# Row sums scaled by a constant: smaller last jobs, an even split of the columns, early stores and two load queues

## Chip, cores, metric

One core of one Trainium2 chip. The metric is the device time of the whole program in microseconds (us); lower is better. Engines have the profile's names: DVE is the vector engine, ACT the scalar engine, SP the sync engine that issues DMAs (a q after a name is an engine's instruction queue). The profile's "span" is the time from the first to the last instruction of one profiled execution, some 1.8 us less than the metric.

## The reference

```python
batch, seq, dim = 32, 512, 1024           # x: 67.1 MB of float32, normal random numbers
def reference(x, multiplier):             # multiplier = 0.5
    return (np.sum(x, axis=-1) * multiplier).astype(np.float32)
```

The 16384 rows of 1024 numbers lie as 128 columns on each of 128 partitions. A column below is one number of the result on each partition, from 128 x 4 KB of input.

## The kernel before

```python
    G = 4
    NT = TPP // G                          # TPP = 128 columns, 32 jobs of four
    x_view = x_flat.rearrange("(p g j) d -> g p j d", p=P, j=G)
    NDVE = (NT * 17) // 32                 # 17 jobs on DVE, 15 on ACT
    BUFS = 10
    # ... pools, sums_dve, sums_act, scaled_dve; order: DVE and ACT jobs in turn, a DVE job last ...
    for g in order:
        x_tile = xpool.tile([P, G, D], fp32)
        nc.sync.dma_start(out=x_tile, in_=x_view[g])
        if g < NDVE:
            nc.vector.reduce_sum(out=sums_dve[:, g * G : (g + 1) * G], in_=x_tile,
                                 axis=mybir.AxisListType.X)
        else:
            for j in range(G):
                c = (g - NDVE) * G + j
                nc.scalar.activation(out=x_tile[:, j, :], in_=x_tile[:, j, :],
                    func=mybir.ActivationFunctionType.Copy, scale=float(multiplier),
                    accum_out=sums_act[:, c : c + 1])
    nc.vector.tensor_scalar(out=scaled_dve, in0=sums_dve, scalar1=float(multiplier),
                            scalar2=None, op0=mybir.AluOpType.mult)
    nc.sync.dma_start(out=out_view[:, : NDVE * G], in_=scaled_dve)
    nc.sync.dma_start(out=out_view[:, NDVE * G :], in_=sums_act)
```

## Time and profile before

| | kernel before |
|---|---|
| time, median of the first 5 runs | 168.96 us (168.85 to 169.38) |
| span of the profiled run (its time: 169.4) | 167.6 us |
| loads | 32 of 2.1 MB, one each 4.895 us |
| last load landed | 160.5 us |
| tail from there to the end of the span | 7.1 us |

The lines of the profile are in the prediction. The way to read them: find the stretch that is set by one resource (here the DMA engines, full from 3 us to 159 us: from 4.2 to 158.5 us at a share of 1.01 and 429 GB/s), then look only at what happens outside it.

### The profile page before, as it was taken

To read this page: it belongs to the slowest core of one execution; us is meant where nothing else is said; L and a number is where in the kernel's file an instruction comes from. 1 tells how busy PE (TensorE), PEld (TensorE's weight loads), DVE (VectorE), ACT (ScalarE), POOL (GpSimd) and SP (SyncE) were. 2 spreads that over 40 slices of the span, in tenths; PEclk is the share of its full clock that TensorE was granted. 3 is DMA by queue.
4 is the path that set the end of the run, shared out by engine and by line. 5 is a ranking of instruction groups with operands and counts; after the bars stand their busy time and mean duration, and the time that the engine had idled before them with its cause. 6 is when DMAs were issued, how large, how long until landed. Compare 5 with 4: busy or idle time off the path is not lost.

```text
span 167.6 us, 253 instructions
## 1 busy us (share of the span) xinstructions
DVE 75.3 (45%) x18; ACT 65.2 (39%) x121; POOL 0.2 (0%) x4
## 2 busy tenths in 40 slices
DVE  0090633709063370906328081552808155180884
ACT  3008155180814518082450906336090633609000
POOL 0000000000000000000000000000000000000000
DMA  5999999999999999999999999999999999999900
GB/s 184 430 430 430 434 422 430 430 434 434 422 430 422 426 434 430 430 422 430 422 432 430 430 426 430 430 422 430 434 426 426 430 426 426 434 426 434 394 8 8
DMA packets 4897, 67.18 MB, mean 401 GB/s; under 512 B 800, under 2 KB 800, under 8 KB 800
## 3 DMA queue, kind: packets, MB, share of 16 engines
q1 hardware_dynamic: 4896, 67.18, 94.6%
q14 instruction: 1, 0.01, 0.0%
HBM read 67.11 MB, written 0.07 MB: 401 GB/s over the span
## 4 chain that ended last, share of the span: by engine, by line
DMA 93%; DVE 3%; SPq 2%; issue 0%
DMA x_tile<-in_x_dram 93%; DVE sums_dve L58 3%; SPq L56 2%; DVE scaled_dve L74 0%
## 5 line engine op out<-in xcount | busy, mean ns | idle before, releaser
L58 DVE TENSOR_REDUCE sums_dve<-x_tile 128x4 f32<-128x4096 f32 x17 | 75.1, 4420 | 89.8 <-DMA x_tile<-in_x_dram 89.8
L66 ACT ACTIVATE x_tile<-x_tile 128x1024 f32<-128x1024 f32 x60 | 62.6, 1043 | 89.1 <-DMA x_tile<-in_x_dram 89.1
L66 ACT ACTIVATION_READ_ACCUMULATOR x_tile<-x_tile 128x1 f32 x60 | 11.2, 186 | 0.0
L66 ACT ACT_TABLE_LOAD x1 | 1.3, 1283 | 0.7 <-PEq L100 0.7
L74 DVE TENSOR_SCALAR scaled_dve<-sums_dve 128x68 f32<-128x68 f32 x1 | 0.2, 196 | 0.0
L100 POOL MEMSET const-bfloat16-1.0<- 128x1 bf16 x1 | 0.1, 101 | 0.0
L100 POOL MEMSET const-uint8-127<- 128x1 uint8 x1 | 0.1, 101 | 0.0
L100 POOL MEMSET const-float32-0.0<- 128x1 f32 x1 | 0.1, 98 | 0.2 <-issue 0.2
L100 POOL MEMSET const-float32-1.0<- 128x1 f32 x1 | 0.1, 98 | 0.0
## 6 DMA issues: line engine op xcount, KB each, us to landing
x_tile<-in_x_dram SPq DMA_DIRECT2D x32, 2048.0 KB, 39.1
out_dram<-scaled_dve SPq DMA_DIRECT2D x1, 34.0 KB, 1.5
out_dram<-sums_act SPq DMA_DIRECT2D x1, 30.0 KB, 5.6
```

Source lines behind the costliest of these rows:

```text
L56: nc.sync.dma_start(out=x_tile, in_=x_view[g])
L58: nc.vector.reduce_sum(out=sums_dve[:, g * G : (g + 1) * G], in_=x_tile, axis=mybir.AxisListType.X,)
L66: nc.scalar.activation(out=x_tile[:, j, :], in_=x_tile[:, j, :], func=mybir.ActivationFunctionType.Copy, scale=float(multiplier), accum_ou ...
L74: nc.vector.tensor_scalar(out=scaled_dve, in0=sums_dve, scalar1=float(multiplier), scalar2=None, op0=mybir.AluOpType.mult,)
L100: nc = _bacc.Bacc("TRN2", target_bir_lowering=False, num_devices=1)
```

## The change

Its intent: shorten what remains after the last load. Each engine gets 64 columns, and its last four come as jobs of 2, 1 and 1 columns. Each engine's sums are stored in two halves, each as soon as it is ready, ACT's from ACT's own DMA queue. Four of the first eight loads are issued by ACT. Cut to its core:

```diff
-    NDVE = (NT * 17) // 32
+    DVE_COLS = TPP // 2
+    ACT_COLS = TPP - DVE_COLS
+    def job_widths(total, bulk):
+        tail = [2, 1, 1] if total >= bulk * 2 + 4 else []
         ...                               # the rest in jobs of four
+    # jobs: DVE and ACT in turn, an ACT column last
+    CHUNK = 32
+    def flush(eng, upto_abs):             # stores 32 columns as soon as they are summed
+        ...
+            if eng == "v":
+                nc.vector.tensor_scalar(out=out_dve[:, lo:hi], in0=sums_dve[:, lo:hi],
+                                        scalar1=mult, scalar2=None, op0=mybir.AluOpType.mult)
+                nc.sync.dma_start(out=out_view[:, lo:hi], in_=out_dve[:, lo:hi])
+            else:
+                nc.scalar.dma_start(out=out_view[:, lo:hi],
+                    in_=sums_act[:, lo - DVE_COLS : hi - DVE_COLS])
     for ji, (eng, c0, w) in enumerate(jobs):
-        nc.sync.dma_start(out=x_tile, in_=x_view[g])
+        dma_eng = nc.scalar if (ji < 8 and ji % 2 == 1) else nc.sync
+        dma_eng.dma_start(out=x_tile, in_=x_cols[:, c0 : c0 + w, :])
         ...
+        flush(eng, done_cols[eng])
-    nc.vector.tensor_scalar(out=scaled_dve, ...)
-    nc.sync.dma_start(out=out_view[:, : NDVE * G], in_=scaled_dve)
-    nc.sync.dma_start(out=out_view[:, NDVE * G :], in_=sums_act)
```

More of the change, by code (lines that the diff above doesn't have):

```diff
@@ L25 @@
     TPP = T // P
-    G = 4
-    NT = TPP // G
-    assert TPP % G == 0
     x_flat = x.rearrange("b s d -> (b s) d")
-    x_view = x_flat.rearrange("(p g j) d -> g p j d", p=P, j=G)
+    x_cols = x_flat.rearrange("(p c) d -> p c d", p=P)
     out_view = out.rearrange("b s -> (b s)").rearrange("(p t) -> p t", p=P)
-    NDVE = (NT * 17) // 32
-    BUFS = 10
-    xpool = ctx.enter_context(tc.tile_pool(name="xpool", bufs=BUFS))
-    spool = ctx.enter_context(tc.tile_pool(name="spool", bufs=1))
-    sums_dve = spool.tile([P, NDVE * G], fp32)
@@ L44 @@
-    sums_act = spool.tile([P, (NT - NDVE) * G], fp32)
-    scaled_dve = spool.tile([P, NDVE * G], fp32)
-    order = []
-    for i in range(max(NDVE, NT - NDVE)):
-        if i < NDVE:
-            order.append(i)
-        if NDVE + i < NT:
-            order.append(NDVE + i)
-    for g in order:
-        x_tile = xpool.tile([P, G, D], fp32)
-        nc.sync.dma_start(out=x_tile, in_=x_view[g])
-        if g < NDVE:
+    DVE_COLS = TPP // 2
+    ACT_COLS = TPP - DVE_COLS
+    def job_widths(total, bulk):
+        tail = [2, 1, 1] if total >= bulk * 2 + 4 else []
+        bulk_cols = total - sum(tail)
+        ws = [bulk] * (bulk_cols // bulk)
+        rem = bulk_cols % bulk
+        if rem:
+            ws.append(rem)
+        return ws + tail
@@ new lines @@
+    GB = 4
+    dve_w = job_widths(DVE_COLS, GB)
+    act_w = job_widths(ACT_COLS, GB)
+    dve_jobs = []
+    c = 0
+    for w in dve_w:
+        dve_jobs.append(("v", c, w))
+        c += w
+    act_jobs = []
+    c = DVE_COLS
+    for w in act_w:
+        act_jobs.append(("a", c, w))
+        c += w
+    jobs = []
+    for i in range(max(len(dve_jobs), len(act_jobs))):
+        if i < len(dve_jobs):
+            jobs.append(dve_jobs[i])
+        if i < len(act_jobs):
+            jobs.append(act_jobs[i])
@@ new lines @@
+    CHUNK = 32
+    xpool = ctx.enter_context(tc.tile_pool(name="xpool", bufs=1))
+    spool = ctx.enter_context(tc.tile_pool(name="spool", bufs=1))
+    sums_dve = spool.tile([P, DVE_COLS], fp32)
+    out_dve = spool.tile([P, DVE_COLS], fp32)
+    sums_act = spool.tile([P, ACT_COLS], fp32)
+    BULK_BUFS = 10
+    SMALL_BUFS = 2
+    mult = float(multiplier)
+    done_cols = {"v": 0, "a": 0}
+    next_flush = {"v": CHUNK, "a": DVE_COLS + CHUNK}
+    def flush(eng, upto_abs):
+        while next_flush[eng] <= upto_abs:
+            hi = next_flush[eng]
+            lo = hi - CHUNK
+            if eng == "v":
+                nc.vector.tensor_scalar(
+                    out=out_dve[:, lo:hi],
+                    in0=sums_dve[:, lo:hi],
+                    scalar1=mult,
+                    scalar2=None,
+                    op0=mybir.AluOpType.mult,
+                )
+                nc.sync.dma_start(out=out_view[:, lo:hi], in_=out_dve[:, lo:hi])
+            else:
+                nc.scalar.dma_start(
+                    out=out_view[:, lo:hi],
+                    in_=sums_act[:, lo - DVE_COLS : hi - DVE_COLS],
+                )
+            next_flush[eng] += CHUNK
@@ L58 @@
+    for ji, (eng, c0, w) in enumerate(jobs):
+        if w == GB:
+            name, nbufs = "x_bulk", BULK_BUFS
+        else:
+            name, nbufs = "x_bulk", BULK_BUFS
+        x_tile = xpool.tile([P, w, D], fp32, name=name, bufs=nbufs)
+        dma_eng = nc.scalar if (ji < 8 and ji % 2 == 1) else nc.sync
+        dma_eng.dma_start(out=x_tile, in_=x_cols[:, c0 : c0 + w, :])
+        if eng == "v":
             nc.vector.reduce_sum(
-                out=sums_dve[:, g * G : (g + 1) * G],
+                out=sums_dve[:, c0 : c0 + w],
@@ L63 @@
         else:
-            for j in range(G):
-                c = (g - NDVE) * G + j
+            for j in range(w):
+                c = c0 + j - DVE_COLS
                 nc.scalar.activation(
@@ L69 @@
                     func=mybir.ActivationFunctionType.Copy,
-                    scale=float(multiplier),
+                    scale=mult,
                     accum_out=sums_act[:, c : c + 1],
                 )
-    nc.vector.tensor_scalar(
-        out=scaled_dve,
-        in0=sums_dve,
-        scalar1=float(multiplier),
-        scalar2=None,
-        op0=mybir.AluOpType.mult,
-    )
-    nc.sync.dma_start(out=out_view[:, : NDVE * G], in_=scaled_dve)
-    nc.sync.dma_start(out=out_view[:, NDVE * G :], in_=sums_act)
+        done_cols[eng] = c0 + w
+        flush(eng, done_cols[eng])
 _INS = ['x', 'multiplier']
```

## The prediction

> **What bounds the kernel now.** I read the page first: the tenths by slice and the chain that ended last.
>
> ```profile
> DVE  0090633709063370906328081552808155180884
> ACT  3008155180814518082450906336090633609000
> DMA  5999999999999999999999999999999999999900
> GB/s 184 430 430 430 434 422 430 430 434 434 422 430 422 426 434 430 430 422 430 422 432 430 430 426 430 430 422 430 434 426 426 430 426 426 434 426 434 394 8 8
> DMA 93%; DVE 3%; SPq 2%; issue 0%
> ```
>
> DMA is full in every slice but the first and the last two (a slice is 4.19 us), and 93% of the chain is loads. DVE and ACT are busy some 45% and 39% and only follow the landings. So there are three stretches: a start without data, a plateau that is set by the bytes, and a tail without data. Only the first and the last can give time back, or the plateau can be made longer. Next I read the end in the timeline, in order of time.
>
> ```profile
> 155.07 0.35 SPq L83 DMA_DIRECT2D out_dram<-sums_act  x1
> 155.62 4.42 DVE L58 TENSOR_REDUCE sums_dve<-x_tile 128x4 f32<-128x4096 f32 x1 [5.37 <-DMA x_tile<-in_x_dram]
> 160.51 4.42 DVE L58 TENSOR_REDUCE sums_dve<-x_tile 128x4 f32<-128x4096 f32 x1 [0.48 <-DMA x_tile<-in_x_dram]
> 164.97 0.20 DVE L74 TENSOR_SCALAR scaled_dve<-sums_dve 128x68 f32<-128x68 f32 x1
> 165.19 0.34 SPq L82 DMA_DIRECT2D out_dram<-scaled_dve  x1
> ```
>
> The last two loads both belong to DVE (17 jobs against ACT's 15), so the last load lands at 160.5 and then one engine alone reduces four columns for 4.42 us, multiplies for 0.20 us and has the sums stored. The page's list of DMA issues gives that store 1.5 us from issue to landing, so it lands at 166.7; the span ends at 167.6, 0.9 us later. The tail from the last landing is 167.6 - 160.5 = 7.1 us.
>
> Then the durations of the two engines, from the groups, and how one ACT job of four columns runs, from the timeline:
>
> ```profile
> L58 DVE TENSOR_REDUCE sums_dve<-x_tile 128x4 f32<-128x4096 f32 x17 | 75.1, 4420 | 89.8 <-DMA x_tile<-in_x_dram 89.8
> L66 ACT ACTIVATE x_tile<-x_tile 128x1024 f32<-128x1024 f32 x60 | 62.6, 1043 | 89.1 <-DMA x_tile<-in_x_dram 89.1
> ```
>
> ```profile
> 150.78 1.06 ACT L66 ACTIVATE x_tile<-x_tile 128x1024 f32<-128x1024 f32 x1 [5.53 <-DMA x_tile<-in_x_dram]
> 151.75 0.19 ACT L66 ACTIVATION_READ_ACCUMULATOR x_tile<-x_tile 128x1 f32 x1
> ...
> 153.92 1.04 ACT L66 ACTIVATE x_tile<-x_tile 128x1024 f32<-128x1024 f32 x1
> 154.86 0.19 ACT L66 ACTIVATION_READ_ACCUMULATOR x_tile<-x_tile 128x1 f32 x1
> ```
>
> One ACT column is over 151.94 - 150.78 = 1.16 us after its start; each further one adds 1.04 us. DVE starts 9.79 us apart (two loads), so one load of 2.1 MB takes 4.895 us, one column of 0.52 MB 1.22 us. Both engines need less for a column than the DMA does for one.
>
> Last, the start and end of the data, in a table of windows.
>
> ```profile
> 1.50:2.00 0.50, 0.00 (x0) 0.50 (x1) 0.00 (x0) 1.00 1.57 295
> 2.50:3.00 0.50, 0.00 (x0) 0.00 (x0) 0.00 (x0) 1.00 0.08 33
> 3.00:3.50 0.50, 0.00 (x0) 0.00 (x0) 0.00 (x0) 1.00 1.01 426
> 158.50:159.00 0.50, 0.50 (x1) 0.00 (x0) 0.00 (x0) 1.00 0.79 332
> 159.00:159.50 0.50, 0.50 (x1) 0.00 (x0) 0.00 (x0) 1.00 0.32 79
> ```
>
> The columns at the end are DMA share and GB/s. Packets begin after 1.5 us, 0.8 us or more after the first issue at 0.73, and the plateau begins at 3.0. In the trace's single packet records the first 16 KB packet of each engine takes 1.0 to 1.6 us and all later ones 0.61 us, so the start loses about 0.7 us beyond the wait for the first packet. Most engines end near 159.1, the slowest at 160.03; its semaphore frees DVE at 160.5.
>
> [...] The trace agrees that there is little to save: an issue takes 0.38 to 0.79 us in the chain, a load 4.895 us. [...]
>
> **The change, part by part.**
>
> *Smaller last jobs, balanced.* Each engine's last four columns become jobs of 2, 1 and 1. The loads end with DVE one column, then ACT one column. Call the last landing T. ACT's two-column job landed about 4.9 us before T and takes 2.2, its next column landed 2.4 before T, so ACT is idle at T: 1.16 us of work, then its store. DVE's last column landed at T - 1.22, is reduced by T, and its multiply (0.20) and store come well before ACT's. Tail: 1.16 (ACT) + 0.04 (two handovers like those between 164.95 and 165.19) + 1.5 (store to landing) + 0.9 (landing to end) = 3.6 us instead of 7.1: -3.5 us.
>
> *Smaller packets.* Columns lie one behind the other, so the rows of the last loads are 8 KB and 4 KB instead of 16 KB. In the packet records a 240-byte packet of the old store comes every 14 ns on one engine and a 16 KB packet every 611 ns; the line through these has a fixed part of 5 ns. Each engine moves 24 more packets for the 4 KB rows and 8 more for the 8 KB rows: 32 x 5 = 0.16 us. Four more loads each bring a 9 ns semaphore packet: 0.04 us. So +0.2 us.
>
> *Early stores.* A first half of each engine's sums (128 rows of 128 bytes) is stored during the plateau. The old ACT store had 8 packets per engine at 14 ns, 0.11 us with its semaphore packet 0.12; two of them +0.25 us on the DMA path. The final stores keep the size class of the old one. The added multiply of 0.2 us lies in DVE's idle time.
>
> *A store on the load queue.* The comparison of instruction orders puts DVE's first store on SP behind 13 SP loads, so that SP stands until DVE has finished job 14 and multiplied: about 4.42 + 0.25 us after that landing. By my walk through the waits, loads 15 and 16 are already issued then, 9.8 us of data. Load 15 is nearly through, load 16 covers 4.9 us; SP needs 0.35 us for the store, 0.45 for the next load and about 1 us to its first packet. About 3 us are to spare: 0.
>
> *Four early loads issued by ACT.* Loads 1 and 3 go out at the start, 5 and 7 (by the order) only after ACT's first eight columns, near 27 us. [...] the first two should land together near 12.5 us. The plateau's bytes and rate stay. Buffers and waits on the eighth load back leave SP always at least two loads ahead: 0. Nothing forces the first data earlier, as SP's first issue is where it was: 0.
>
> Sum: -3.5 + 0.2 + 0.25 = -3.05 us; 168.96 - 3.05 = 165.9 us, or -1.8%.
>
> **The rivals.**
>
> *The two queues hide the start.* If a second queue's packets overlap the slow first packet of each engine, up to 0.7 us comes back: 165.2 us, over 2% faster. For it: 1.0 to 1.6 us against 0.61 looks like latency, which overlap can hide. Against it: later packets are back to back with no gap, the engine appears to work on one at a time, and SP alone had several loads queued behind the first one.
>
> *The stores or the ordering open a bubble.* If the DVE store in the SP queue starves the loads, or if the small packets cost far more beside loads than alone, some 1 to 4 us are lost: 166.9 to 169.9 us. For it: SP does stand, and every load that waits for a slot can pass that on. Against it: 3 us of slack, and the old ACT store already went through behind a load with 14 ns a packet.
>
> *ACT's store is dearer than SP's.* ACT issued no DMA before. If its issue to landing is 2 to 2.5 us instead of 1.5, the time is 166.4 to 166.9. No view speaks to it.
>
> **Range and chances.** The mechanism of the tail is nearly certain; what is open is about half a microsecond each in the start, the plateau and ACT's store. 165.9 us, range 165.1 to 166.8. The 2% line is at 165.6, only 0.3 us below the centre, so faster is 0.35, same 0.63, slower 0.02.
>
> **What would show it.** Right: the last activation starts near 160.9 and is one column; ACT's store is the last thing issued, near 162.1; the span ends near 164.5; the plateau still shows about 428 GB/s with no slice below 9 tenths but the ends; DVE's first reduce starts near 12.5. Wrong: a slice in the middle (about 80 us) with less DMA; a last landing above 161.5 (plateau longer than the 0.45 us that I add) or below 160.3 (start gained); an ACT store with more than 2 us to landing; DVE's chain ending after ACT's.

## The result, and the profile after

The changed kernel took 165.86 us (median of 8 runs, 165.59 to 166.01); the kernel before took 169.29 us in the same rounds (15 runs, 168.85 to 169.49). The ratio is 0.980, with a 95% interval of 0.9788 to 0.9811. It lies on the 2% line, so the verdict between "faster" and "same" is unclear. Ratios here are the mean time of one kernel's fast runs over that of the other's of the same rounds, so they are not quite the ratio of the medians quoted. The time is the predicted 165.9 almost to the digit, but that flatters the prediction: the kernel before was 0.33 us slower in these rounds than in the five runs I started from. The drop is 3.4 us, predicted were 3.05.

The page of the changed kernel's profile, with busy tenths of each engine by slice and the chain that ended last:

```profile
DVE  0008247906346090642808246090642708145541
ACT  3007236009056708145090642708145090632872
DMA  5999999999999999999999999999999999999990
GB/s 192 432 440 420 436 428 440 424 424 436 420 432 428 424 428 432 436 420 422 440 420 425 436 424 428 436 420 432 432 420 432 428 432 428 424 436 404 412 372 8
DMA 93%; DVE 3%; SPq 2%; ACT 1%; issue 0%; ACTq 0%
```

The DMA row ends with one empty slice instead of two: the tail is shorter. In the middle no slice falls below nine tenths, so the early stores opened no bubble. The GB/s of slices 37 and 38 (404 and 412) show the small rows of the last loads; experiment 4, which has none, shows 432 in both. The end, from the timeline (start, duration, engine and line; in brackets how long the engine had been idle and what ended that):

```profile
159.06 1.22 DVE L113 TENSOR_REDUCE sums_dve<-x_bulk 128x1 f32<-128x1024 f32 x1 [1.34 <-DMA x_bulk<-in_x_dram]
160.31 0.18 DVE L88 TENSOR_SCALAR out_dve<-sums_dve 128x32 f32<-128x32 f32 x1
160.36 1.06 ACT L121 ACTIVATE x_bulk<-x_bulk 128x1024 f32<-128x1024 f32 x1 [1.38 <-DMA x_bulk<-in_x_dram]
160.52 0.34 SPq L95 DMA_DIRECT2D out_dram<-out_dve  x1
161.32 0.19 ACT L121 ACTIVATION_READ_ACCUMULATOR x_bulk<-x_bulk 128x1 f32 x1
161.54 0.35 ACTq L97 DMA_DIRECT2D out_dram<-sums_act  x1
```

ACT's last column starts at 160.36, at the landing, and its store is issued 1.18 us later; the span ends at 163.8, 2.3 us after that. The tail is 163.8 - 160.4 = 3.4 us, against 7.1 before. DVE, which ended the kernel before, is now done a microsecond ahead of ACT. Its one-column reduce takes 1.22 us; that it would be over at the last landing was my estimate, as the kernel before has only reduces of four columns (4.42 us).

The stand of SP that the order of instructions announced (its queue holds back loads until DVE has finished the sums that it must store) is there too (a wait of 24.4 us for DVE in SP's list of waits), in the timeline near 81 us:

```profile
81.33 0.18 DVE L88 TENSOR_SCALAR out_dve<-sums_dve 128x32 f32<-128x32 f32 x1
81.54 0.35 SPq L95 DMA_DIRECT2D out_dram<-out_dve  x1
81.94 13.36 SPq L110 DMA_DIRECT2D x_bulk<-in_x_dram  x7
```

SP's next load leaves 0.4 us after the store, while load 16 is still in the queue; the window from 80 to 85 us has a DMA share of 1.00 and 426 GB/s. The stand costs nothing.

What does not fit is the last landing: 160.4 in place of the 160.9 that the prediction worked out. Every term that was to lengthen the plateau is therefore in doubt, and the experiments take them one by one.

### The profile page after: what moved, and what is told of

Same layout as the page of the kernel before. It is cut to its first block, busy times and chain, and to the rows that moved or that the text cites. A ratio compares the mean times of both kernels' runs of the same rounds, so it can differ in the third digit from the quotient of the medians.

```text
span 163.8 us, 268 instructions
## 1 busy us (share of the span) xinstructions
DVE 71.4 (44%) x20; ACT 69.7 (43%) x129; POOL 0.2 (0%) x4
## 2 busy tenths in 40 slices
DMA packets 5761, 67.19 MB, mean 410 GB/s; under 512 B 1152, under 2 KB 1152, under 8 KB 1664
## 4 chain that ended last, share of the span: by engine, by line
DMA 93%; DVE 3%; SPq 2%; ACT 1%; issue 0%; ACTq 0%
DMA x_bulk<-in_x_dram 93%; DVE sums_dve L113 3%; SPq L110 1%; ACT x_bulk L121 1%; SPq L95 0%; DVE out_dve L88 0%; ACTq L121 0%
## 5 line engine op out<-in xcount | busy, mean ns | idle before, releaser
L113 DVE TENSOR_REDUCE sums_dve<-x_bulk 128x4 f32<-128x4096 f32 (+2 forms) x18 | 71.0, 3946 | 89.0 <-DMA x_bulk<-in_x_dram 89.0
L121 ACT ACTIVATE x_bulk<-x_bulk 128x1024 f32<-128x1024 f32 x64 | 66.8, 1044 | 90.1 <-DMA x_bulk<-in_x_dram 90.1
L121 ACT ACTIVATION_READ_ACCUMULATOR x_bulk<-x_bulk 128x1 f32 x64 | 11.9, 186 | 0.0
```

What stands on the lines that cost most here:

```text
L113: nc.vector.reduce_sum(out=sums_dve[:, c0 : c0 + w], in_=x_tile, axis=mybir.AxisListType.X,)
```

## The experiments

They ran in three groups of four, each group on one chip together with the kernel before (medians there 169.09, 169.14 and 169.21 us). Between groups I compare ratios only. Below, "jump" means: the last load's landing signal comes from 16 DMA engines (the trace has 16 semaphore updates for each load); the jump is how far the slowest comes behind the second slowest, from the trace's semaphore records. "Spread" is from the first engine's to the slowest's.

### 1. The small last jobs, with the even split, alone

Based on the changed kernel:

```diff
-        dma_eng = nc.scalar if (ji < 8 and ji % 2 == 1) else nc.sync
+        dma_eng = nc.sync
-    CHUNK = 32
+    CHUNK = 64
```

> The small, balanced last jobs alone: all loads from SP, one store per engine at the end (ACT's still from ACT). Theory (the tail gives everything, the early stores cost 0.25 us, two load queues gain 0.2 us at the start): ratio to the kernel before about 0.98, time within 0.2 us of the changed kernel's 165.9; tail from last landing to end 3.5 us. Rival (the two queues or the early stores carry a real part of the gain): above 166.6 us. In the profile the first load should land near 8.4 us, and 16 loads' worth of data about 0.2 us later than in the changed kernel.

Measured: 166.27 us, ratio 0.9836 (0.9822 to 0.9849). Most of the gain is here: 2.8 us against this group's 169.09, where the changed kernel had 3.4 against its own. It fits neither line that I had drawn: it is 0.4 us over the changed kernel's 165.9, not within 0.2, and under the rival's 166.6; and 16 loads' worth of data landed at 81.48 us, not later than the changed kernel's 81.61. The remaining 0.4% of time looks like a gain from the other parts, but the profile says otherwise. DVE's starts in this kernel, from the timeline:

```profile
76.61 4.42 DVE L113 TENSOR_REDUCE sums_dve<-x_bulk 128x4 f32<-128x4096 f32 x1 [5.37 <-DMA x_bulk<-in_x_dram]
87.02 4.42 DVE L113 TENSOR_REDUCE sums_dve<-x_bulk 128x4 f32<-128x4096 f32 x1 [5.99 <-DMA x_bulk<-in_x_dram]
```

Two loads lie between the starts, 9.79 us everywhere else; here it is 10.41. The kernel before has the same step, a smaller one, at the same place in its timeline:

```profile
76.86 4.42 DVE L58 TENSOR_REDUCE sums_dve<-x_tile 128x4 f32<-128x4096 f32 x1 [5.37 <-DMA x_tile<-in_x_dram]
87.08 4.42 DVE L58 TENSOR_REDUCE sums_dve<-x_tile 128x4 f32<-128x4096 f32 x1 [5.80 <-DMA x_tile<-in_x_dram]
```

In both, an 8 KB packet on the instruction queue (q14 in the list of DMA queues) runs at 85.2 to 85.3 us for 0.31 us. I read it so: it falls on one of the 16 engines, and that engine stays late to the end, as if each engine had a fixed share of each load (the trace does not name the engine of a packet). A load packet just after it, at 85.60 us in the kernel before, takes 0.99 us, where all others after 4.5 us stay below 0.70. The jump is about 0.05 us before it in this kernel and 0.62 to 0.67 us from it to the end (0.1 and 0.46 in the kernel before; in the changed one, where the packet comes at 75.6 us, 0.1 before it, 0.20 at the next landing, then 0.04 to 0.09). This was in no part of my prediction, and it became the theory for the second group.

### 2. All loads from SP, the rest as changed

```diff
-        dma_eng = nc.scalar if (ji < 8 and ji % 2 == 1) else nc.sync
+        dma_eng = nc.sync
```

> The changed kernel with all loads from SP, the rest as it is. Theory (two queues gain only about 0.2 us of the cold start): 0.1 to 0.3 us slower than the changed kernel, 166.1 us. Rival of the prediction (two queues hide the whole slow first packet, 0.7 us): 166.5 us or more. Third (they do nothing): 165.9.

Measured: 166.18 us, ratio 0.9834 (0.9821 to 0.9848); the changed kernel had 0.980. The time fits the theory's 166.1, but not for its reason: the start shows no gain from two queues. The last landing of the first 14 loads' worth of data is a mark that lies before any fetch or store: at 71.75, 71.81 and 71.77 us in three profiles of the changed kernel, at 71.87 in experiment 3 and 71.96 in experiment 4; with one queue at 71.69, 71.73, 71.71 and 71.80 in four kernels of this tail, and at 71.95, 71.94 and 71.84 in the kernel before. The groups overlap. Two queues bring the start no gain that shows here. Against experiment 1, which differs only in the early stores, there is no difference either: 0.9834 to 0.9836. What stays open is the time: 0.9834 lies clear above the three ratios of the changed kernel (0.9795 to 0.9808). In this kernel's profile, its fastest run, the last landing is that of the changed kernel (160.32 against 160.28 to 160.63 us); its other runs were up to 0.5 us slower. The fetch can make such a difference, but no profile of a slower run shows that it did.

### 3. Late stores

```diff
-    CHUNK = 32
+    CHUNK = 64
```

> The changed kernel with one store per engine at the end. Theory (an early store is 0.12 us of DMA time on the path and gives nothing back): 0.2 to 0.3 us faster, 165.6 us, and no stand of SP at 81 us. Rival (early stores shorten the last store): 0 to 0.3 us slower. The final stores should land 1.4 to 1.5 us after issue with 256-byte rows as with 128-byte rows.

Measured: 166.09 us, ratio 0.9821 (0.9808 to 0.9835). My theory expected 165.6; it fails. Leaving out the early stores brings no gain: the ratio is 0.2% above that of the changed kernel rather than 0.15% below, with intervals that overlap. The final stores with 256-byte rows take 1.5 us, as before.

### 4. Even split, no small jobs

```diff
-        tail = [2, 1, 1] if total >= bulk * 2 + 4 else []
+        tail = []
```

> The changed kernel with 16 jobs of four columns for each engine and no small ones: balance alone. Theory (the size of the last job is what counts): the last load is ACT's four columns, 4.27 us of work instead of 1.16, so 3.1 us longer, less 0.2 us of small packets: 168.8 us, ratio to before 0.995 to 1.0. Rival (the balance of 16 to 16 instead of 17 to 15 is a large part of the gain): 167.5 us or less.

Measured: 168.92 us, ratio 0.9994 (0.9981 to 1.0008), as the theory said. The even split, the early stores and the two queues together are worth nothing without the small last jobs. The end, from this kernel's timeline:

```profile
160.22 1.06 ACT L121 ACTIVATE x_bulk<-x_bulk 128x1024 f32<-128x1024 f32 x1 [5.50 <-DMA x_bulk<-in_x_dram]
...
163.35 1.04 ACT L121 ACTIVATE x_bulk<-x_bulk 128x1024 f32<-128x1024 f32 x1
164.51 0.35 ACTq L97 DMA_DIRECT2D out_dram<-sums_act  x1
```

From landing to store 4.29 us, against 1.18 in the changed kernel. The difference, 3.1 us, less some 0.3 for the small packets (below), is nearly the whole gain of the change: in this group 2.7 to 2.9 us lie between this kernel and experiments 2 and 3. ACT had waited 5.5 us for that load, so it was not short of time; the load was too large to be the last.

### 5. The changed kernel again

No edit.

> The changed kernel as it is, on the chip of the next three. Theory: 165.9 us, 165.6 to 166.1 from run to run, ratio 0.980 to 0.982. The profile's instruction fetch (one 8 KB packet on the fetch queue near 76 us) adds 0 to 0.6 us to the spread of the last load's landing over the 16 DMA engines; its size differs from the first profile's 0.1.

Measured: 165.61 us (165.54 to 165.66), ratio 0.9795 (0.978 to 0.9809), at the lower end of what was expected. Its jump at the last load is 0.12 us against 0.07 in its first profile; I had expected a clearer difference.

### 6. Few instructions on ACT

Experiment 1's kernel with 100 columns on DVE:

```diff
-    DVE_COLS = TPP // 2
+    DVE_COLS = 100
-    for i in range(max(len(dve_jobs), len(act_jobs))):   # in turn
+    for i in range(6):
+        jobs += dve_jobs[4 * i : 4 * i + 4] + [act_jobs[i]]
+    for i in range(3):
+        jobs += [dve_jobs[24 + i], act_jobs[6 + i]]
     # and one store per engine, of its own number of columns
```

> The small-tail kernel with late stores and all loads on SP, but DVE takes 100 columns and ACT 28, so ACT runs under half the instructions. Fetch theory (the fetch in mid-run is ACT's next instructions, and it delays one DMA engine for the rest of the run): no packet on the fetch queue in mid-run, the spread of a load's landing over the engines stays at 0.6 to 0.7 us from the first load to the last, the last load lands 0.2 to 0.6 us earlier than in the first run of this tail, time 165.5 to 165.8 us and within 0.15 us from run to run. Rival (the fetch comes with time or belongs to another engine): a fetch near 85 us as before, no gain, 166.2 us; DVE's load of 100 columns must not show, as 24 x 4.42 us is 106 us.

Measured: 165.76 us (165.63 to 165.88), ratio 0.9804 (0.9789 to 0.9818), against 0.9836 for experiment 1 with the same tail, same queues and same late stores. DVE is busy for 111 us instead of 71 and does not show in the time. The spread is 0.5 to 0.6 us from the first load to the last. The fetch has not vanished: it came late, just before ACT's last column. The list of queues for the window from 158 to 160 us:

```profile
q1 hardware_dynamic: 148, 0.51, 63.8%
q14 instruction: 1, 0.01, 1.0%
```

So it follows ACT's progress through its program, not the clock; in this kernel it comes when the loads are nearly over. The last load lands at 160.14 us, 0.56 earlier than in experiment 1, within the 0.2 to 0.6 expected. The range from run to run, 0.25 us, is wider than the 0.15 I expected.

### 7. More instructions on ACT

Experiment 1's kernel, with two extra instructions of one element for each of ACT's first 60 columns (in the trace most of a job's run after its last column):

```diff
+                for _ in range(2 if c0 + w <= TPP - 4 else 0):
+                    nc.scalar.activation(out=dummy[:, 1:2], in_=x_tile[:, j, 0:1],
+                        func=mybir.ActivationFunctionType.Copy, scale=mult)
```

> The small-tail kernel with late stores and all loads on SP, with two extra ACT instructions of one element after each of the first 60 columns (results unchanged). They fit into ACT's idle time. Fetch theory: the fetch comes earlier, near 45 us, and there are two or three of them within the loads; each delays one engine by up to 0.3 us; the time is 0 to 0.6 us above the 166.27 us of this tail, depending on whether they fall on the same engines. Rival (the count of instructions has nothing to do with it): one fetch near 85 us, same time.

Measured: 166.64 us (166.53 to 166.74), ratio 0.9854 (0.9837 to 0.987): clear above experiment 6's 0.9804, and above experiment 1's 0.9836 with intervals that overlap. There are two fetches within the loads now, as the list of DMA queues up to 160 us counts them; the packet records have them at 41.1 and 119.5 us. The second one shows in DVE's starts:

```profile
q14 instruction: 2, 0.02, 0.0%
```

```profile
116.28 4.42 DVE L114 TENSOR_REDUCE sums_dve<-x_bulk 128x4 f32<-128x4096 f32 x1 [5.37 <-DMA x_bulk<-in_x_dram]
126.76 4.42 DVE L114 TENSOR_REDUCE sums_dve<-x_bulk 128x4 f32<-128x4096 f32 x1 [6.06 <-DMA x_bulk<-in_x_dram]
```

10.48 us instead of 9.79. The jump goes from 0.02 to 0.37 at the first and to 1.07 at the second: so the second, it seems, fell on the engine that the first had made the last. The last column starts at 161.28 where experiment 6 has 160.22, and the span is 1.1 us longer. ACT's extra work does not explain it: ACT has a backlog at its last jobs of 2 and 1 columns, but is done with it and idle for 1.18 us before the last load lands. Between the two fetches lie 78.4 us, eight of ACT's jobs of 16 instructions, 128 in all. In all fourteen profiles the first fetch within the program comes after 51 to 69 of ACT's recorded instructions, be that at 41 us or at 160.

### 8. Seven stores beside the loads

Experiment 1's kernel, with ACT's sums stored in eight pieces:

```diff
-    CHUNK = 64
+    CHUNK = {"v": 64, "a": 8}
```

> The small-tail kernel with all loads on SP, DVE's store at the end, but ACT's sums stored in eight pieces of eight columns, seven of them beside the loads. Theory (an early store costs its 8 packets per engine, 0.12 us): 7 x 0.12 = 0.8 us slower than the 166.27 us of this tail, 167.1 us. Rival (a small store beside loads costs far more than alone): 168 us or more. Third (it hides in the gaps of the engines): below 166.6 us.

Measured: 165.83 us (165.77 to 165.96), ratio 0.9809 (0.9794 to 0.9824). My theory expected 167.1, and the third possibility came true: seven more stores do not lengthen the loads. In the median over the engines the last load lands at 159.84 us, in experiment 1 at 159.83. The time is even lower than experiment 1's, which fits the fetch's jump, 0.26 here against 0.64. From the list of queues and of DMA issues:

```profile
q10 hardware_dynamic: 1152, 0.03, 0.4%
out_dram<-sums_act ACTq DMA_DIRECT2D x8, 4.0 KB, 9.1
```

The 1152 packets on ACT's queue take 0.4% of the 16 engines' time, and yet nothing is lost; how the engines manage that, the trace does not tell. In the changed kernel's packet records the 128 rows of ACT's first store start between 89.53 and 93.88 us, spread over 4.3 us among load packets of 0.61 us, which looks like one row of the store to a load packet on each engine (8 rows each). For larger rows it is not quite nothing. Take the time from the landing of the 14th load to that of the last, each as the mean over the 16 engines, so that one late engine hardly counts: it is 88.39 us here (four of the seven stores lie in it), 88.43 in experiments 1 and 3 without an early store, but 88.49 to 88.51 in experiment 2 and the three profiles of the changed kernel, which have two early stores with 128-byte rows. Experiment 4, with two and no small packets, has 88.21, the kernel before 88.14 to 88.15. Two such stores cost 0.06 to 0.08 us, not 0.25. A store of ACT that runs beside loads lands after 9.1 us in place of 1.5. What waited for that was the issue of later loads (these stores are 6% of this run's chain; in the changed kernel SP waited 8.0 us for one), and the DMA row of the page stays at nine tenths.

### 9. The changed kernel a third time

No edit.

> The changed kernel once more, beside the half-column kernel on one chip. Theory: 165.6 to 165.9 us; the spread of the last load's landing over the DMA engines is 0.8 to 0.9 us, as in its two profiles so far, if the engine that the fetch falls on belongs to the kernel; anything from 0.7 to 1.3 if it changes from launch to launch.

Measured: 165.95 us (165.88 to 166.04), ratio 0.9808 (0.9794 to 0.9821). The jump is 0.41 us and the last column starts at 160.71. So the engine that the fetch falls on does not belong to the kernel: three profiles of one kernel had jumps of 0.07, 0.12 and 0.41. They come from different groups, so whether the launch or the chip decides is not shown.

### 10. The last column in two halves

Experiment 6's kernel; DVE's last column is moved ahead of ACT's last two, and the very last column comes as two loads of half a column:

```diff
-    for i in range(3):
-        jobs += [dve_jobs[24 + i], act_jobs[6 + i]]
+    jobs += [dve_jobs[24], act_jobs[6], dve_jobs[25], dve_jobs[26], act_jobs[7]]
     ...
+    nc.sync.dma_start(out=x_last[:, :, :half], in_=x_cols[:, last : last + 1, :half])
+    nc.sync.dma_start(out=x_last2[:, :, :half], in_=x_cols[:, last : last + 1, half:])
+    # ACT: first half into sums_act[:, k]; DVE: second half into part, then
+    nc.vector.scalar_tensor_tensor(out=sums_act[:, k : k + 1], in0=part, scalar=mult,
+        in1=sums_act[:, k : k + 1], op0=mybir.AluOpType.mult, op1=mybir.AluOpType.add)
+    nc.sync.dma_start(out=out_view[:, DVE_COLS:], in_=sums_act)
```

> The kernel with few ACT instructions, its last column loaded in two halves: ACT sums the first, DVE the second and adds. Theory (the time after the last landing is the size of the last job and what cannot be cut: 2.4 us of store and end): DVE's half column 0.69 us and the addition 0.2 us in place of ACT's 1.16: 0.2 us faster than the kernel with few ACT instructions at the same last landing, less 0.05 to 0.1 us of smaller packets; 165.5 to 165.7 us. Rival (the end is bound by something else, as DVE's handovers): no gain.

Measured: 165.35 us (165.28 to 165.39), ratio 0.9771 (0.9758 to 0.9785), against 0.9808 for the changed kernel on the same chip. It is the best version, 0.6 us ahead of the changed kernel beside it, better than the 165.5 to 165.7 us expected. Its end, from the timeline:

```profile
160.28 0.69 DVE L144 TENSOR_REDUCE part<-x_bulk 128x1 f32<-128x512 f32 x1 [1.12 <-DMA x_bulk<-in_x_dram]
160.61 0.19 ACT L137 ACTIVATION_READ_ACCUMULATOR x_bulk<-x_bulk 128x1 f32 x1
161.08 0.16 DVE L145 SCALAR_TENSOR_TENSOR sums_act<-part,sums_act 128x1 f32<-128x1 f32 x1
161.26 0.34 SPq L153 DMA_DIRECT2D out_dram<-sums_act  x1
```

From landing to store 0.98 us instead of 1.18: the 0.2 us of the theory. The rest of its lead comes from the last landing (160.28 against 160.71), with its instruction fetch at 160.4 us, after the last load. Its runs lie within 0.11 us.

### 11. and 12. The kernel before, two more profiles

No edit.

> The kernel before, one more profile. Fetch theory: the span follows the spread of the last load's landing over the DMA engines: with the engine that is last anyway hit (spread 1.1 to 1.2 us, as in the first profile) 167.5 us, with another one hit (0.7 us) 167.1 us. Rival: spans vary while the spread stays the same.

> As the run before it, a second profile: span 167.1 with a spread of 0.7 us, 167.5 with 1.1 us.

Measured: 169.29 and 169.25 us, spans 167.5 and 167.5, spreads 1.05 and 1.01 us, jumps 0.30 and 0.36. Both had the fetch on a late engine, so they agree with the theory's upper case (1.1 us of spread and 167.5); a run of the kernel before without a jump was not caught in a profile. That its range of 168.8 to 169.5 us is the fetch's work therefore stays a likely reading, not one shown.

## Why the prediction was right

*The bound and the tail: right.* The loads stayed the bound, and the tail shrank from 7.1 to 3.4 us; 3.6 was predicted. The terms: ACT's column to its store 1.18 us (1.16 and a handover), store and end together 2.3 (2.4). Experiment 4 shows the cause: with everything else of the change and a last job of four columns, nothing is gained.

*Smaller packets: right.* Predicted +0.2 us. In the changed kernel's timeline the ACT job before the eight last columns starts at 150.31, the last column at 160.36; that is 10.05 us for eight columns, against two loads of 4.895 us, so +0.26. (In the mean over the engines, as in experiment 8: 88.43 in experiments 1 and 3 against 88.15 before, +0.28.) The records give 162.8 ns for a 4 KB packet, so a little more of fixed cost than the line through two sizes had.

*Early stores: a cost that was sized more than three times too large.* The prediction put "+0.25 us on the DMA path" for two of them. Measured are 0.06 to 0.08 us (experiment 8); experiment 8's seven with shorter rows show no cost, and experiments 1 and 2, with none and with two, have the same ratio. I had read the 14 ns a packet from a store that ran behind an engine's last load, and added it where load packets were in flight.

*SP's stand, and four loads from ACT: right, zero each,* as far as the profiles show (experiment 2 leaves 0.3% in the times open). One detail was off: loads 5 and 7 left at 23.0 us, when ACT began the second of its jobs (its first activation starts at 22.99), and not near 27 when it had finished. The first two loads landed together, at 13.02 and 13.19 us where the kernel before has 8.35 and 13.20 (DVE's first start 13.0, predicted 12.5): from 3 to 13 us the packet records have 128 load packets of SP's queue and 135 of ACT's.

*Missing from the sum: the instruction fetch.* One fetch adds 0 to 0.7 us to the last landing in the kernels here that run 60 or more activations on ACT beside the loads. Experiment 6 moves it by instruction count, experiment 7 doubles it; the landing and the time go with it. In the first pair of profiles the jump at the last load was 0.46 us in the kernel before and only 0.07 in the changed one, which hid the +0.26 of small packets and made the last landing look earlier.

Over three profiles each, the last landing (start of the job that follows it) is 160.42 us before and 160.50 after, so the last landing moved by 0.1 us on average and not by 0.45. That is partly luck: in the mean over the engines the stretch after the 14th load did get 0.35 us longer (88.50 against 88.15), but the slowest engine came 0.2 us less far behind that mean, and the first 14 loads landed 0.14 us earlier in the mean (71.40 against 71.54; experiments 1 and 2 with one queue have 71.42, so it is not the second queue, and why stays open). With the tail's 3.7 this gives 3.6 us of span, and the medians differ by 3.3 to 3.5 (the profiled runs of the kernel before, at 169.4, 169.3 and 169.25 us, lay above the medians of their groups).

*The rivals.* Two queues that hide the start: no (experiment 2, by the landings). A bubble from the stores: no. A dear store from ACT: no, 1.5 us as from SP.

Open: which of the 16 engines a fetch falls on, why small stores beside loads are nearly free, and whether the fetch alone makes experiment 2 slower than the changed kernel.

## What to carry to other kernels

In these kernels, which only stream data, what remained after the last landing was the last job (1.18 us to its store for one column, 4.29 for four) and a store that cost about the same everywhere: 2.2 to 2.5 us from its issue to the end of the span in all fourteen profiles. So make the last jobs small on every engine, and stop when their small rows cost the DMA as much as they save (here 0.26 us for eight columns, against 3.1 saved). Balance, a second load queue and early stores gave nothing that showed here; do not expect more of them unless a view shows a stretch in which the DMA stands. When two kernels differ by less than 0.5%, look at the landing signal of single DMA engines: one instruction fetch on the slowest of them was a difference of that size here (a jump of 0.46 us against 0.07 in the first pair of profiles), and which run it hit was chance as far as these profiles show.
